# Later transposes, an earlier lambda and three later weight casts at the joint between the first feed-forward block and the token mixer

## The chip, the cores and the metric

The kernel runs on one core of one Trainium2 chip. The metric is device time in microseconds (us) of one execution. The kernel before took 925.24 us (median of three runs, from 924.72 to 927.66).

## The reference, cut to what matters

One layer in float32 on 512 tokens of width 1024: a feed-forward block (SwiGLU, 2816 hidden columns), a token mixer (attention), a second feed-forward block, and a last RMS norm. In four of the mixer's heads two softmaxes are combined with a scalar, `lam`. The mixer's input is the first block's output, normed over the 1024 columns; its first step is the projection to queries, keys and values.

```
def swiglu(x, w_gate, w_up, w_down):
    return (jax.nn.silu(x @ w_gate) * (x @ w_up)) @ w_down
...
    proj = h @ w_in
...
    lam = (jnp.exp(jnp.sum(lq1.astype(f32) * lk1.astype(f32)))
           - jnp.exp(jnp.sum(lq2.astype(f32) * lk2.astype(f32))) + lam0)
...
        a = p[:, :, 0] - lam * p[:, :, 1]
...
        x = x + 0.5 * swiglu(rmsnorm(x, ffn1_norm[layer]),
                             ffn1_w_gate[layer], ffn1_w_up[layer], ffn1_w_down[layer])
        x = x + token_mixer(rmsnorm(x, mix_norm[layer]), w_in[layer], w_out[layer],
...
    return rmsnorm(x, final_norm)
```

## The kernel before, in words

**Precision.** Every large product is made of three matmuls of fp32r parts (`mm3`, L160 to L162): high part by high part, the activation's low part by the weight's high part, and high by the weight's low part. So each weight and each activation is split on the way: ScalarE (ACT in the profile) casts a high part `h`, and VectorE (DVE) subtracts it from the original for a low part `l`. TensorE (PE) needs both before it can use the operand.

**The first block's down projection** turns tokens to the outside (the result has 128 tokens on the partitions). Of the 22 blocks of 128 hidden rows the last sixteen are taken as eight pairs, in two groups of four pairs, each multiplied Strassen-like in seven products instead of eight. The second group (unit `("t", 1)`, four row pairs p = 0 to 3) runs the products `a11, a22, s2, a12, s1, s3, s4` in this order, each with four weight tiles. For each weight tile a small planner (`block_events`) pushes timed events on a heap: the load (L478, L484, L481), a sum if the product needs one (`total`, L406), the cast (`high`, L443) four steps ahead of the product and the low part (`low`, L447) three steps ahead; a step is the time of one tile's matmuls, 1.41 us in the plan. The heap's order is the order of the instructions on the engines; nothing is moved by a scheduler, so each engine executes its list in order and stands when an entry has to wait. In the same stretch the last hidden rows' own parts are still made (names `g0a`, `g1a`, and `h0a` to `h6a`, where `h5a` and `h6a` are the high and low part that product `a22` needs of the last row pair).

**The joint** is written by hand in `seam`. Its four token tiles tt = 0 to 3 each go through: two times nine matmuls of the first six row blocks, for the right half of the columns (`plain_mm`, out `pc`), an add to the stream (`add`, L1321, DVE), a sum of squares (`squared`, L1324, ACT), the norm's factor (`mean` and `root_part`, L1287 to L1295), a scaling (`scaled`, out `y`: one half on ACT L1332, one on DVE L1334), and eight 128x128 transposes on PE (`turn`, L1342, out `xt`). Tiles 0 and 1 fill four PSUM banks (side 0, 256 tokens), tiles 2 and 3 four banks (side 1). After the second turn of a side, `split` reads each bank twice per row block k = 0 to 7: ACT makes `xh` (L1281), DVE `xl` (L1283). The pool `mm` has four banks in all, so the first turn of side 1 writes the banks that side 0's `split` reads: bank k // 2 is free once both readers of its two row blocks are done.

Among the turns stand sixteen **chunks**: chunks 0 to 7 multiply side 0 by the first two units of query and key weights (`pq`, `pk`; chunk c reads row blocks 2(c mod 4) and the next, with unit c // 4), chunks 8 to 15 the same for side 1. A chunk is twelve matmuls. Each runs `step(c)`, which also issues what a table holds for that step (`put(step, rank, function)`): loads and splits of later weights (`raw_vw`, L1449 and L1453), the evacuation of finished units (`evac_now` for unit 0 at step 11: L1553, L1217, L1556, L1220, L1610; `casts_k`, `evac_k` and so on for unit 1 from step 16), the scores of the attention from step 16 on (`sc`, L1659 and L1660, in two PSUM banks in turn, each read by DVE at L1662), and the scalar **lambda**: `lam_load` (a GpSimd DMA of `lt` into a buffer that `y` of tile 2 held, L1395) and `lam` (two DVE operations on `lt`, an Exp on ACT with its table load at L1404, five small DVE operations).

Before the change the turn of tile 2 stands ahead of chunk 1, that of tile 3 ahead of chunk 4 with side 1's `split` behind it; lambda's load stands in step 6 and its arithmetic in step 14. Because chunk bodies come after their step's events of rank under 10, "in step 14" puts lambda's DVE and ACT work behind the evacuation of unit 0.

Of the kernel before, what the change touches and what calls it, by code (L numbers as in the profile page):

```python
# [57 lines left out]
          "seven": (("a11", "w", "b11"), ("a22", "z", "t4"), ("s2", "w", "t2"), ("a12", "v", "b21"),  # L58
                    ("s1", "z", "t1"), ("s3", "v", "t3"), ("s4", "z", "b22")),
          "fresh": ("a11", "a22", "s3"),  # L60
          "s1": ((8, 9, 10, 11),) * 2, "s3": (tuple(t[0] for t in PAIR_SLOTS),) * 2,
          "a22": (("bc", "ob", "ob", "sq"),) * 2, "a12": (("bc", "ob", "ob", "sq"),) * 2,
          "ahead": {"s1": ((26, 23, 20, 17),) * 2, "s3": ((-1.7, -2.7, -3.7, -4.7),) * 2,
                    "a11": ((11, 10, 9, 8), (11, 10, 5.9, 5.8)), "a22": ((8, 7.5, 7, 6.5), (6.5, 6.3, 3.8, 0.5)),
                    "a12": ((-1.6, -2.6, -3.6, -4.6),) * 2}},
    "b": {"plain": 4, "pairs": ((4, 6, 8, 10), (12, 14, 16, 18, 20)),
          "sets": {4: (28, 29, 30, 31, 32, 33, 34), 6: (35, 36, 37, 38, 39, 40, 41),
# [19 lines left out]
STEP, TILES_STEP = 1410, 5440  # L87
# [12 lines left out]
def tile_macaron(ctx: ExitStack, tc, xs, xT, wf, wgu1, wst1, wdg1, wqk, wvw, wv, wo, wgu2, wst2,  # L100
# [17 lines left out]
    def mm_bank(nm):  # L118
        return pp.tile([P, S], F32, tag="mm", name=nm, bufs=4)
# [39 lines left out]
    def mm3(po, wh, wl, mh, ml, first, last, on=False):  # L159
        T.matmul(po, wh, mh, start=first, stop=False, skip_group_check=on)  # L160
        T.matmul(po, wh, ml, start=False, stop=False, skip_group_check=on)  # L161
        T.matmul(po, wl, mh, start=False, stop=last, skip_group_check=on)  # L162
# [78 lines left out]
    def ffn(wgu, wst, wdg, n0, n1, norm, early, res, nm, hooks, first=None,  # L241
# [99 lines left out]
        shape = TURNED[nm]  # L341
# [171 lines left out]
        def at(time, rank, f, *a):  # L513
            count[0] += 1
            heapq.heappush(events, (time, rank, count[0], f, a))
# [335 lines left out]
        def block_events(t):  # L851
            u, o, p = ops[t]
            now = starts[t]
            if o[0] in shape["ahead"]:
                at(starts[begin[u]] - shape["ahead"][o[0]][u[1]][p] * STEP, 2.2, block_load, u, o[0], p)
            elif o[0] in ("a12", "a22"):
                at(now - 8 * STEP, 1.5, block_load, u, o[0], p)
            if final is not None and (u[1], o[0]) == (1, "s4"):
                now = starts[begin[u]] + (TURNED_KEPT[p] + 5) * STEP
            if o[0] in ("s2", "s4"):  # L860
                at(now - 5 * STEP, 2, total, t)
            at(now - 4 * STEP, 3, high, t)
            at(now - 3 * STEP, 2.5, low, t)
            if t == begin[u] and u[1] == 1 and final is not None:
                at(now + 2 * STEP, 1, final, "begin", now + 2 * STEP, put, None)
# [200 lines left out]
        for j in range(j0, n1):  # L1066
# [9 lines left out]
            for hf in range(2):  # L1076
                wh, wl = get_w(wgu[j, hf], f"gu{nm}{j}_{hf}")
                for kk in range(4):
                    k = hf * 4 + kk
                    for c, pt in ((0, pg), (1, pu)):  # L1080
                        o = kk * 256 + c * P
# [39 lines left out]
    with tc.manual_schedule(engines={mybir.EngineType.DVE, mybir.EngineType.Activation}):  # L1121
        for t in range(4):
            raw = wp.tile([P, 1024], F32, tag="raw", name=f"raw_f{t}")
            h, l = w_place()
            for kk in range(2):
                k = 2 * t + kk
                c = slice(kk * 512, kk * 512 + 512)
# [82 lines left out]
    def number(n, tt):  # L1210
        return fin[:, n * NQ + tt:n * NQ + tt + 1]

    def first_sum(tt):
        V.tensor_scalar(number(2, tt), number(0, tt), 1.0 / D, EPS, op0=ALU.mult, op1=ALU.add)
# [82 lines left out]
    def seam(step):  # L1297

        todo, now, ys, ts, cb = [], [0.0], {}, {}, {}

        def ev(t, f, *a):
            todo.append((t, len(todo), f, a))

        def pe(cost, f, *a):
            ev(now[0], f, *a)
            now[0] += cost

        def plain_mm(tt, hf):
            ah, al = closing["tiles"]
            if hf == 0:  # L1310
                tag = ("s", "s", "t", "t")[tt]
                cb[tt] = pp.tile([P, S], F32, tag=tag, name=f"pc{tt}", bufs=2)[:]
            c = slice(tt * P, (tt + 1) * P)
            for j in range(3 * hf, 3 * hf + 3):
                h, l = closing[j // 2]
                w = slice(j % 2 * 512, (j % 2 + 1) * 512)
                mm3(cb[tt], ah[j][:, c], al[j][:, c], h[:, w], l[:, w], j == 0, j == PLAIN - 1)

        def add(tt):
            y = x[4 + tt]  # L1320
            V.scalar_tensor_tensor(y, cb[tt], 0.5, y, op0=ALU.mult, op1=ALU.add)  # L1321

        def squared(dh, tt):
            A.activation(sq[:], x[4 * dh + tt], AF.Square, accum_out=number(dh, tt))  # L1324
            if dh == 0:
                first_sum(tt)

        def scaled(dh, tt):
            y = tp.tile([P, S], F32, tag=("ob", "ptb")[tt % 2], name=f"y{dh}{tt}")
            ys[dh, tt] = y  # L1330
            if dh == 0:
                A.activation(y[:], x[tt], AF.Copy, scale=number(6, tt))  # L1332
            else:
                V.tensor_scalar_mul(y[:], x[4 + tt], number(6, tt))  # L1334

        def turn(tt):
            side = tt // 2
            if tt % 2 == 0:
                ts[side] = [mm_bank(f"xt{side}{i}") for i in range(4)]
            for k in range(KD):  # L1340
                o = k % 2 * HS + tt % 2 * P
                T.transpose(ts[side][k // 2][:, o:o + P], ys[k // 4, tt][:, k % 4 * P:(k % 4 + 1) * P], ident[:])  # L1342

        def chain(tt):
            t = now[0]
            ev(t + 0.1, add, tt)
            ev(t + 0.8, squared, 1, tt)
            ev(t + 1.6, mean, tt)
            ev(t + 2.0, root_part, tt)
            for dh in range(2):  # L1350
                ev(t + 2.7, scaled, dh, tt)

        def split(side, t):
            for k in range(KD):
                ev(t + 0.1 + 0.42 * k, gathered, "h", 1, side, k, ts)
                ev(t + 0.55 + 0.42 * k, gathered, "l", 1, side, k, ts)

        ev(-1, V.tensor_scalar_mul, sm[:, KD:2 * KD], sm[:, KD:2 * KD], 2.0)
        for t, tt in ((0.2, 0), (0.9, 1), (2.9, 2), (3.6, 3)):
            ev(t, squared, 0, tt)  # L1360
        for t, low, u, hf, c, n in ((1.6, 2.7, 0, 0, 0, 1024), (8.1, 11.4, 0, 1, 0, 1024), (11.8, 12.5, 1, 0, 0, 512),
                                    (12.4, 13.1, 1, 0, 512, 512), (21.5, 22.1, 1, 1, 0, 512),
                                    (22.1, 22.7, 1, 1, 512, 512)):
            ev(t, early_high, u, hf, c, n)
            ev(low, early_low, u, hf, c, n)
        ev(0.3, early_load, 1, 0)
        ev(3.5, early_load, 1, 1)
        for tt in range(NQ):
            pe(2.05, plain_mm, tt, 0)
            if tt > 1:  # L1370
                pe(0.8, turn, tt - 2)
            if tt == 3:
                split(0, now[0])
            pe(2.05, plain_mm, tt, 1)
            chain(tt)
        for c in range(16):
            if c in (1, 4):
                pe(0.8, turn, 2 + c // 4)
            if c == 4:
                split(1, now[0])  # L1380
            pe(1.36, step, c)
        for _, _, f, a in sorted(todo, key=lambda e: (e[0], e[1])):
            f(*a)
# [46 lines left out]
    def put(t, rank, f, *a):  # L1430
        at.setdefault(t, []).append((rank, f, a))
# [8 lines left out]
    loaded, ready, later = {}, {}, []  # L1440
# [447 lines left out]
    for i, f in enumerate(bounds):  # L1888
        put(22 + i, 9, f)

    put(6, 4, lam_load)
    put(14, 4, lam)
    for n, c in enumerate((0, 0, 2)):
        put(c, 0, load, n)
    for n, c in enumerate((3, 5)):
# [3 lines left out]
    def step(t):  # L1899
# [12 lines left out]
        if later:  # L1912
            hi_, lo_ = later.pop(0)
            hi_()
            lows.append(lo_)

    seam(step)
    for t in range(16, max(len(chunks), max(at) + 1)):
        step(t)
# [252 lines left out]
```

## Time and profile before

| | |
|---|---|
| timed runs | 924.72, 925.24, 927.66 us |
| the profiled execution | 923.94 us |
| its span, first to last instruction | 922.2 us |
| mean granted TensorE clock | 0.999 |
| TensorE busy | 911.1 us (99%), 5796 matmuls |
| VectorE busy | 716.1 us (78%) |
| ScalarE busy | 551.2 us (60%) |
| GpSimd busy | 93.3 us (10%) |
| the joint (chunks 0 to 15 and the turns among them) | from 344.1 to 371.1 us |
| the second down group begins | 287.6 us |

The profile's rows of a timeline read: start in us, duration in us, engine, line of the kernel, operation, out<-in, shape, count, and in brackets the idle time of the engine just before it with what ended it. PEld is TensorE's loading of the stationary operand, which runs beside the matmuls. SPq is the queue of the engine that issues most loads. Matmuls are pipelined, so what a matmul costs is the time from its start to the next one's start (0.23 us at 512 columns, 0.12 us at 256), and not the duration in its row.

### The profile page before, as it was taken

The page shows a single profiled execution, that of the slowest core. Times are in us where ns is not written, and L with a number is a line of the kernel's source. Part 1 is how long each engine was busy: PE and PEld are TensorE (multiplying, and loading weights), DVE is VectorE, ACT ScalarE, POOL GpSimd, SP SyncE. Part 2 cuts the span into 40 slices and gives each one's busy share as a digit, 9 for nine tenths or more (in the row PEclk, how much of TensorE's full clock was granted, in tenths as well). Part 3 has the DMA queues.
Part 4 walks back from the last instruction along what each step waited for, and adds up shares of the span by engine and source line. Part 5 has one row for each costly group of instructions (what it writes and reads, how often), then busy time and mean ns, then how long its engine had stood idle before and what let it go on. Part 6 is the DMA issues. An engine that isn't in the chain of part 4 may idle for free.

```text
span 922.2 us, 15983 instructions
## 1 busy us (share of the span) xinstructions
PE 911.1 (99%) x5796; PEld 820.7 (89%) x5796; DVE 716.1 (78%) x1486; ACT 551.2 (60%) x1160; POOL 93.3 (10%) x117
## 2 busy tenths in 40 slices
PE   9999999999999999999999999999999999999997
PEld 7888999889998889888989878989999889999885
DVE  7797887687888964857866546797887877988786
ACT  7454665445657564655776675656666446666563
POOL 0001111112120000000000000011221012211100
PEclk9999999999999999999999999999999999999999
DMA  7456679567895642324444204365798269787722
GB/s 256 125 140 158 181 181 261 137 153 199 188 229 156 168 137 76 92 92 116 137 111 118 69 23 138 93 149 161 186 240 214 81 182 236 206 187 208 194 69 91
DMA packets 65807, 141.52 MB, mean 153 GB/s; under 512 B 7552, under 2 KB 8064, under 8 KB 65728
## 3 DMA queue, kind: packets, MB, share of 16 engines
q1 hardware_dynamic: 50736, 113.02, 38.0%
q0 software_dynamic: 14992, 27.48, 18.4%
q8 instruction: 45, 0.74, 0.3%
q14 instruction: 34, 0.28, 0.1%
HBM read 135.20 MB, written 2.14 MB: 149 GB/s over the span
## 4 chain that ended last, share of the span: by engine, by line
PE 92%; DVE 4%; ACT 2%; issue 1%; DMA 0%; DVEq 0%; SPq 0%; ACTq 0%
PE pt L162 5%; PE pt L160 5%; PE pt L161 5%; PE pwo L160 2%; PE pwo L161 2%; PE pwo L162 2%; PE pq L160 2%; PE pua L160 2%; PE pua L162 2%; PE pua L161 2%; PE pq L161 1%; PE pq L162 1%; PE pk L160 1%; PE pk L162 1%; PE pk L161 1%; PE pp L160 1%
## 5 line engine op out<-in xcount | busy, mean ns | idle before, releaser
L1665 ACT ACTIVATE pr<-pr,mx 128x128 f32<-128x128 f32 (+3 forms) x64 | 36.0, 563 | 36.4 <-DVE mx L1662 36.1
L1662 DVE CUSTOM_DVE_ANT_0 pr<-sc,strip 128x128 f32<-128x128 f32 (+3 forms) x64 | 30.5, 489 | 21.8 <-PE sc L1660 21.3
L379 POOL DMA_DIRECT2D s1bg<-wst_dram x10 | 8.7, 865 | 352.8 <-DVE fin L1294 239.1
L535 DVE SCALAR_TENSOR_TENSOR x<-pt,x 128x512 f32<-128x512 f32 x50 | 32.8, 687 | 14.1 <-PE pt L162 11.7
L447 DVE TENSOR_TENSOR w<-s2b,w 128x512 fp32r<-128x512 f32 x38 | 26.1, 687 | 6.0 <-ACT w L443 6.0
L443 ACT CAST w<-s2b 128x512 fp32r<-128x512 f32 x38 | 23.6, 620 | 6.4 <-DVE s2b L411 6.1
L160 PE MATMUL pwo<-w,mh 128*128 128x512 f32 x64 | 25.9, 405 | 0.0
L447 DVE TENSOR_TENSOR w<-s2a,w 128x512 fp32r<-128x512 f32 x30 | 20.6, 687 | 6.5 <-ACT w L443 6.5
L161 PE MATMUL pwo<-w,mh 128*128 128x512 f32 x64 | 25.0, 391 | 0.0
L162 PE MATMUL pwo<-w,ml 128*128 128x512 f32 x64 | 25.0, 391 | 0.0
L443 ACT CAST w<-s2a 128x512 fp32r<-128x512 f32 x30 | 18.6, 620 | 8.0 <-DVE s2a L411 8.0
L443 ACT CAST w<-raa 128x512 fp32r<-128x512 f32 x24 | 14.5, 621 | 13.8 <-PE pt L162 5.6
L162 PE MATMUL pwgb<-xh,w 128*128 128x256 f32 x80 | 22.7, 284 | 0.0
L1453 DVE TENSOR_TENSOR w<-raw_qk,w 128x512 fp32r<-128x512 f32 x24 | 16.4, 687 | 8.1 <-ACT w L1449 8.0
L160 PE MATMUL pwgb<-xh,w 128*128 128x256 f32 x80 | 22.5, 281 | 0.0
L161 PE MATMUL pxgb<-ttb,w 128*128 128x256 f32 x80 | 22.5, 281 | 0.0
L161 PE MATMUL pwgb<-xl,w 128*128 128x256 f32 x80 | 22.5, 281 | 0.0
L1659 PE MATMUL sc<-k,q 128*128 128x128 f32 (+3 forms) x64 | 20.7, 325 | 0.8 <-DVE mx L1662 0.8
L1660 PE MATMUL sc<-l,q 128*128 128x128 f32 (+3 forms) x64 | 20.4, 322 | 0.0
L162 PE MATMUL pwub<-xh,w 128*128 128x256 f32 x72 | 20.3, 281 | 0.0
L161 PE MATMUL pwub<-xl,w 128*128 128x256 f32 x72 | 20.3, 281 | 0.0
L160 PE MATMUL pwub<-xh,w 128*128 128x256 f32 x72 | 20.3, 281 | 0.0
(728 smaller groups left out, 3868.3 us busy)
## 6 DMA issues: line engine op xcount, KB each, us to landing
raw_qk<-wqk_dram SPq DMA_DIRECT2D x12, 512.0 KB, 3.5
raw0bg<-wst_dram SPq DMA_DIRECT2D x10, 512.0 KB, 5.5
raw0bu<-wst_dram SPq DMA_DIRECT2D x9, 512.0 KB, 5.9
raw_gua<-wgu_dram SPq DMA_DIRECT2D x8, 512.0 KB, 3.7
raw0ag<-wst_dram SPq DMA_DIRECT2D x8, 512.0 KB, 5.1
strip<-bias_rows SPq DMA_DIRECT2D x16, 256.0 KB, 3.6
raw_wo<-wo_dram SPq DMA_DIRECT2D x8, 512.0 KB, 3.5
raw0au<-wst_dram SPq DMA_DIRECT2D x7, 512.0 KB, 6.7
```

The source lines that it names most:

```text
L160: T.matmul(po, wh, mh, start=first, stop=False, skip_group_check=on)
L161: T.matmul(po, wh, ml, start=False, stop=False, skip_group_check=on)
L162: T.matmul(po, wl, mh, start=False, stop=last, skip_group_check=on)
L379: nc.gpsimd.dma_start(t[:], b, accum_op=ALU.add)
L443: A.copy(made[t][0], source(t))
L447: V.tensor_tensor(l, source(t), h.bitcast(F32), op=ALU.subtract)
L535: V.scalar_tensor_tensor(o, a, f, b, op0=ALU.mult, op1=op1)
L1453: V.tensor_tensor(l[:, c:c + 512], raw[:, c:c + 512], h[:, c:c + 512].bitcast(F32), op=ALU.subtract)
L1659: T.matmul(ps[:, :w], qs[:, qi], ks[:, :w], start=True, stop=False)
L1660: T.matmul(ps[:, :w], qs[:, qi], ls[:, :w], start=False, stop=True)
L1662: V.tensor_tensor_reduce(out=pi, in0=ps[:, :w], in1=st["b"][m][:, w - 1::-1], op0=ALU.add, op1=ALU.min, scale=1.0, scalar=3.0e38, accum_ou ...
L1665: A.activation(pi, pi, AF.Exp, scale=-1.0, bias=st["mx"][:, m, i:i + 1], accum_out=st["ls"][:, m, i:i + 1])
```

## The change

Four things move; nothing is added and nothing taken away.

```
+          "later": ((("t", 1), "a11", 2), (("t", 1), "a11", 3), (("t", 1), "a22", 3)),
...
-                    "a12": ((-1.6, -2.6, -3.6, -4.6),) * 2}},
+                    "a12": ((-1.6, -2.6, -3.6, -4.6), (-1.6, -2.6, -3.6, -5.2))}},
...
+            if (u, o[0], p) in shape.get("later", ()):
+                now += STEP
             at(now - 4 * STEP, 3, high, t)
             at(now - 3 * STEP, 2.5, low, t)
...
         for c in range(16):
-            if c in (1, 4):
-                pe(0.8, turn, 2 + c // 4)
-            if c == 4:
+            if c in (3, 5):
+                pe(0.8, turn, 2 + c // 5)
+            if c == 5:
                 split(1, now[0])
             pe(1.36, step, c)
...
-    put(6, 4, lam_load)
-    put(14, 4, lam)
+    put(4, 4, lam_load)
+    put(9, 4, lam)
```

The turn of tile 2 goes from ahead of chunk 1 to ahead of chunk 3, that of tile 3 from ahead of chunk 4 to ahead of chunk 5, and `split(1)` with it. Lambda's load goes from step 6 to step 4, its arithmetic from step 14 to step 9. In the second down group the casts and low parts of `a11` p = 2 and 3 and of `a22` p = 3 go one step later, and the load of `a12` p = 3, which uses the buffer (`sq`) of `a22` p = 3, 0.6 steps later. Line numbers of the changed kernel are 1 higher from the table on and 3 higher behind `block_events`.

On PE, in the joint: the last matmul of chunk 0, the turn of tile 2 (`y_3695` and `y_3697` are its two halves, `xt_3743` to `xt_3746` the four banks), and the first of chunk 1, before.

```order
L162 MATMUL pk_3722<-xh_79,wql_3569 128x256
L1342 MATMUL xt_3743<-ident,y_3695 128x128 x2
L1342 MATMUL xt_3744<-ident,y_3695 128x128 x2
L1342 MATMUL xt_3745<-ident,y_3697 128x128 x2
L1342 MATMUL xt_3746<-ident,y_3697 128x128 x2
L160 MATMUL pq_3721<-xh_80,wqh_3568 128x256
```

The same turn on PE in the changed kernel stands between the last matmul of chunk 2 (row block 5 is `xh_83`) and the first of chunk 3 (row block 6 is `xh_84`).

```order
L163 MATMUL pk_3722<-xh_83,wx 128x256
L1345 MATMUL xt_3782<-ident,y_3695 128x128 x2
L1345 MATMUL xt_3783<-ident,y_3695 128x128 x2
L1345 MATMUL xt_3784<-ident,y_3697 128x128 x2
L1345 MATMUL xt_3785<-ident,y_3697 128x128 x2
L161 MATMUL pq_3721<-xh_84,wqh_3617 128x256
```

So the 24 matmuls of chunks 1 and 2 went ahead of it.

On ACT, from side 1's last `xh` on: the evacuation of unit 0 (`q_3943` to `l_3948`), lambda's table load and Exp, and the first casts of unit 1's keys (`k_4034`, `k_4035`) and the first softmax exponential, before.

```order
L1281 ACTIVATE xh_85<-xt_3746,x_104 128x256
L1553 ACTIVATE q_3943<-pq_3721 64x512
L1217 CAST k_3945<-pk_3722 64x512 x2
L1610 CAST l_3947<-l_3947 64x512
L1553 ACTIVATE q_3944<-pq_3721 64x512
L1217 CAST k_3946<-pk_3722 64x512 x2
L1610 CAST l_3948<-l_3948 64x512
L1404 ACT_TABLE_LOAD
L1404 ACTIVATE ls<-ls 128x2
L1217 CAST k_4034<-pk_3821 64x512
L1217 CAST k_4035<-pk_3821 64x512
L1665 ACTIVATE pr_3977,ls_3980<-pr_3977,mx_3979 128x128
```

The same stretch on ACT in the changed kernel.

```order
L1284 ACTIVATE xh_85<-xt_3785,x_104 128x256
L1407 ACT_TABLE_LOAD
L1407 ACTIVATE ls<-ls 128x2
L1556 ACTIVATE q_3954<-pq_3721 64x512
L1220 CAST k_3956<-pk_3722 64x512 x2
L1613 CAST l_3958<-l_3958 64x512
L1556 ACTIVATE q_3955<-pq_3721 64x512
L1220 CAST k_3957<-pk_3722 64x512 x2
L1613 CAST l_3959<-l_3959 64x512
L1220 CAST k_4034<-pk_3815 64x512
L1220 CAST k_4035<-pk_3815 64x512
L1668 ACTIVATE pr_3988,ls_3991<-pr_3988,mx_3990 128x128
```

The table load and the Exp went from between the two units' evacuations to ahead of both; on DVE lambda's seven operations went the same way, from ahead of the first L1662 to right behind side 1's last `xl`.

On DVE, in the second down group: a sum for `s2` (`raa`), the low part of `a22` p = 3 (`w<-sq`), and the parts `h4a` and `h6a` of the last row pair, before.

```order
L406 TENSOR_TENSOR raa_3025<-sCa_2792,raa_3025 128x512
L447 TENSOR_TENSOR w<-sq,w 128x512
L715 TENSOR_TENSOR h4a_3319<-g0a_3063,h3a_3258 128x512
L406 TENSOR_TENSOR raa_3136<-sCa_2859,raa_3136 128x512
L447 TENSOR_TENSOR w<-raa_3025,w 128x512
L1191 TENSOR_TENSOR ac<-ac,rb 16x16
L715 TENSOR_TENSOR h6a_3335<-g1a_3096,h5a_3294 128x512
```

The same rows on DVE in the changed kernel.

```order
L407 TENSOR_TENSOR raa_3025<-sCa_2792,raa_3025 128x512
L716 TENSOR_TENSOR h4a_3317<-g0a_3063,h3a_3258 128x512
L407 TENSOR_TENSOR raa_3136<-sCa_2859,raa_3136 128x512
L448 TENSOR_TENSOR w<-sq,w 128x512
L448 TENSOR_TENSOR w<-raa_3025,w 128x512
L1194 TENSOR_TENSOR ac<-ac,rb 16x16
L716 TENSOR_TENSOR h6a_3335<-g1a_3096,h5a_3293 128x512
```

The low part from `sq` went two places back, and `h6a` kept its place. The two `a11` low parts likewise went three and two places back further up. On ACT the cast of `sq` went behind three bias operations (L1187), the cast of `h5a` and two copies of the finished product `a11` (L523), the cast of `a11` p = 3 behind two casts of the last rows' parts; on SP the load of `a12` p = 3 changed places with the load that followed it.

## The prediction

> **What bounds the kernel now.** First the page's busy line, then all waits of TensorE (PE).
>
> ```profile
> PE 911.1 (99%) x5796; PEld 820.7 (89%) x5796; DVE 716.1 (78%) x1486; ACT 551.2 (60%) x1160; POOL 93.3 (10%) x117
> ```
>
> ```profile
> PE warm L1112 <- POOL ones_d L1106: 1.0, 1, 1.0
> PE xt L1342 <- DVE fin L1287: 0.9, 1, 0.9
> PE pga L1157 <- ACT w L1137: 0.9, 1, 0.9
> PE sc L1659 <- DVE mx L1662: 0.8, 1, 0.8
> PE xt L1342 <- DVE xl L1283: 0.6, 1, 0.6
> ```
>
> PE is the bound nearly everywhere. Five waits make all of its idle time, 4.2 us; two lie at the program's start, out of the change's reach. The other three lie in the joint and at the first scores, 2.3 us by this list. Work on other engines counts only where PE ends up waiting. A "busy" PE also includes stalls that the pipelined ends cover, so I read the price from the starts of PE's rows: the turn of tile 2, which begins where chunk 0 ends, the next chunk's first matmul, and for comparison the turn of tile 3, three chunks on.
>
> ```profile
> 345.81 0.60 PE L1342 MATMUL xt<-ident,y 128*128 128x128 f32 x4
> 347.06 0.41 PE L1342 MATMUL xt<-ident,y 128*128 128x128 f32 x2 [0.65 <-DVE xl L1283]
> 348.36 0.41 PE L1342 MATMUL xt<-ident,y 128*128 128x128 f32 x2 [0.89 <-DVE fin L1287]
> 348.52 0.36 PE L160 MATMUL pq<-xh,wqh 128*128 128x256 f32 x1
> ...
> 352.93 1.03 PE L1342 MATMUL xt<-ident,y 128*128 128x128 f32 x8
> 353.72 0.36 PE L160 MATMUL pq<-xh,wqh 128*128 128x256 f32 x1
> ```
>
> The turn of tile 3 costs 353.72 - 352.93 = 0.79 us, that of tile 2 348.52 - 345.81 = 2.71: **1.92 us too many**. What does it wait for? The third bank, then the fourth. DVE's side of it (`xl` of side 0, with tile 3's `add` between) and ACT's last `xh`:
>
> ```profile
> 343.87 1.66 DVE L1283 SCALAR_TENSOR_TENSOR xl<-xt,x,xh 128x256 fp32r<-128x256 f32 x4 [1.06 <-ACT xh L1281]
> 345.44 0.68 DVE L1321 SCALAR_TENSOR_TENSOR x<-pc,x 128x512 f32<-128x512 f32 x1
> 346.04 0.87 DVE L1283 SCALAR_TENSOR_TENSOR xl<-xt,x,xh 128x256 fp32r<-128x256 f32 x2
> 347.33 0.88 DVE L1283 SCALAR_TENSOR_TENSOR xl<-xt,x,xh 128x256 fp32r<-128x256 f32 x2 [0.43 <-ACT xh L1281]
> ```
>
> ```profile
> 346.22 0.63 ACT L1324 ACTIVATE sq<-x 128x512 f32<-128x512 f32 x1 [0.56 <-DVE x L1321]
> ...
> 346.85 0.46 ACT L1281 ACTIVATE xh<-xt,x 128x256 fp32r<-128x256 f32 x1
> ```
>
> The first six `xl` end at 346.91 and the third pair of transposes starts at 347.06; the last two end at 348.21 and the fourth pair starts at 348.36. The reader that frees a bank lets PE in 0.15 us later (the name `fin` in the list is the operation after it).
>
> **The turn, 1.92 us.** The end at 348.21 hangs on ACT's square at 346.22 and that on `add` at 345.44, whose matmuls ended before chunk 0. None of it depends on where the turn stands, so in the new place the same bank is free at 348.36. A chunk costs (352.93 - 348.52) / 3 = 1.47 us. Chunks 1 and 2, now first, start at 345.81 and end at 348.75. Chunk 1 reads `xl` 2 and 3, ready at 345.53; chunk 2 reads 4 and 5 from 347.28, ready at 346.91; chunk 3 reads 6 and 7 after the turn, ready at 348.21. So the turn starts at 348.75 with every bank free, its first by 4 us, its last (used about 0.4 into the turn) by 0.8, and ends at 349.54. Chunks 3 and 4 follow, and the turn of tile 3 stands at 352.48. Its `y` comes from here:
>
> ```profile
> 349.19 0.72 ACT L1332 ACTIVATE y<-x,fin 128x512 f32<-128x512 f32 x1 [0.68 <-DVE fin L1295]
> ...
> 353.34 1.20 ACT L1281 ACTIVATE xh<-xt,x 128x256 fp32r<-128x256 f32 x3 [1.35 <-PE xt L1342]
> ```
>
> It is there at 349.91. I count the whole 1.92 as gained. What is late next? Side 1's split has one chunk less of cover. ACT starts it 0.41 after the turn (353.34 against 352.93), so at 352.89; eight `xh` at 0.40 and the one weight cast now between them (0.5) end at 356.6, and DVE, 0.9 behind at first, needs eight at 0.40 and two low parts at 0.6: about 358. Chunk 8 starts at 353.27 + 3 x 1.47 = 357.68 and needs only the first two pairs, chunk 11 at 362.1 the last. About 3 us of cover stay: 0.
>
> **Lambda, 1.04 us.** The first scores (`sc`), with PE's rows around the wait:
>
> ```profile
> 377.30 0.40 PE L1518 MATMUL pvw<-w,xh 128*128 128x512 f32 x1
> 378.46 0.44 PE L1659 MATMUL sc<-k,q 128*128 128x384 f32 x1 [0.76 <-DVE mx L1662]
> 378.74 0.34 PE L1660 MATMUL sc<-l,q 128*128 128x384 f32 x1
> 378.91 0.40 PE L1516 MATMUL pvw<-w,xh 128*128 128x512 f32 x1
> ```
>
> From 377.30 to 378.46 are 1.16 instead of the 0.23 of such a matmul, then 0.28 for the first `sc` where the second, of the same shape, takes 0.17: 0.93 + 0.11 = 1.04 lost. PE wants the bank that DVE reads in L1662, in this string:
>
> ```profile
> 370.61 0.29 DVE L1401 TENSOR_TENSOR lp<-lt 128x128 f32<-128x128 f32 x1
> ...
> 373.74 0.29 DVE L1662 CUSTOM_DVE_ANT_0 pr<-sc,strip 128x128 f32<-128x128 f32 x1
> ...
> 378.32 0.08 DVE L1662 DVE_READ_ACCUMULATOR2_ANT mx<- 128x1 f32 x1
> ```
>
> ```profile
> 371.25 1.28 ACT L1404 ACT_TABLE_LOAD   x1
> ...
> 372.78 1.19 ACT L1217 CAST k<-pk 64x512 fp32r<-64x512 f32 x2
> ```
>
> Lambda holds DVE from 370.61 to 373.7 and ACT from 371.25 to 372.78. Without it the casts of `k`, whose bank PE fills four chunks after chunk 11 (below: 365.15 + 4 x 1.47 = 371.0), start at about 371.3, 1.5 earlier. DVE's first L1662 moves by more, since its score follows chunk 15 at once, and what stands between it and 378.32 are ACT's casts and DVE's answers to them, all 1.5 earlier. A string moved by 1.5 clears a wait of 0.93. Relative to PE I count 1.04 gained. In its new place lambda falls into this hole:
>
> ```profile
> 365.15 0.59 ACT L1553 ACTIVATE q<-pq 64x512 fp32r<-64x512 f32 x1 [7.75 <-PE pq L162]
> 365.78 0.68 DVE L1556 SCALAR_TENSOR_TENSOR q<-pq,q 64x512 fp32r<-64x512 f32 x1 [6.54 <-ACT q L1553]
> ```
>
> ACT starts unit 0's evacuation there when PE is through chunk 11, in the new kernel at 365.15 - 1.92 = 363.2. Lambda needs 3.1 from about 358, so it ends near 361.1, with 2 us to spare.
>
> ```profile
> 346.98 0.58 POOL L1395 DMA_DIRECT2D lt<-lams_dram  x1 [40.62 <-PE xt L1342]
> ...
> DMA to landing us min/median/max: 3.5/3.5/3.5
> ```
>
> Its input waits for `y` of tile 2 to be read by PE, then near 349.2, and lands 3.5 later, at 352.7; nothing else is queued on GpSimd there.
>
> **The three casts, 0.** In the second down group PE's weight load stands 0.39 us once, for a residual that DVE makes late (the group's first row, then PEld's, DVE's and ACT's):
>
> ```profile
> 287.60 0.40 PE L160 MATMUL pt<-w,h0a 128*128 128x512 f32 x1
> ```
>
> ```profile
> 297.74 0.19 PEld L162 LDWEIGHTS pt<-w,h6a 128*128 128x128 f32 x1 [0.39 <-DVE h6a L715]
> ```
>
> ```profile
> 294.52 0.69 DVE L447 TENSOR_TENSOR w<-sq,w 128x512 fp32r<-128x512 f32 x1
> ```
>
> ```profile
> 294.47 1.04 ACT L523 COPY pt<-pt 128x512 f32<-128x512 f32 x2
> ```
>
> All that stood ahead of `h6a` on DVE still does, and DVE works there without a gap, so it ends when it did. The new risk is that `w<-sq`, on DVE now two places of 0.6 later, at 295.7, waits for ACT's cast behind the copies. With that cast gone from ahead of them the copies can start when PE is through `a11`, near 287.6 + 4 x 1.4 = 293.2, and the cast is done at 295.0. Were the copies to keep their time and end at 295.5, the cast would end at 296.1, and `h6a` and PE come 0.4 later. Bounds: -0.39 (the wait goes) to +0.4; I take 0, since the rows ahead of `h6a` are the same. The load that shares `sq` leaves 0.8 later on SP, behind one load more:
>
> ```profile
> 295.62 0.38 SPq L481 DMA_DIRECT2D sq<-wdg_dram  x1
> ...
> 302.79 0.62 ACT L443 CAST w<-sq 128x512 fp32r<-128x512 f32 x1 [1.28 <-DMA sq<-wdg_dram]
> ```
>
> Its product starts near 287.6 + 15 x 1.4 = 308.6, 4 us after the cast would now end: 0.
>
> **The sum.** 1.92 + 1.04 = 2.96. The profiled execution took 923.94 (span 922.2 and 1.74 around it), so 920.98; the median of the timed runs lies 1.30 higher, 925.24, and gives **922.3**. Behind that I see nothing that takes it back or adds to it, for DVE has caught up with PE soon after in the kernel before, too:
>
> ```profile
> 388.62 0.56 DVE L1662 CUSTOM_DVE_ANT_0 pr<-sc,strip 128x384 f32<-128x384 f32 x1 [0.92 <-PE sc L1660]
> ```
>
> **The rivals.** (a) *The scores still wait.* If the string at 371 to 378 hangs on PE's own rhythm (DVE's `q` and weight parts) rather than on lambda, only the turn is gained: 923.3. For it: DVE has work in every slice there. Against it: 1.5 of shift for a wait of 0.93. 0.12. (b) *The wait moves along with the turn*, the change not doing what it says, if the banks' readers slipped behind the two chunks: only lambda's 1.04, 924.2. Against it the chain of rows above, which ends at 348.21 without a link to chunks 1 or 2. 0.05. (c) *Slower: lambda's input comes late.* ACT is in order, so an Exp without its input holds unit 0's evacuation. With lambda's last 2.5 us behind the landing, it harms nothing up to a landing at about 360.7; scores need that evacuation 1.5 later, and from there PE stands one to one. To eat 2.96 the load would have to land after 365, 16 us after its issue against 3.5; at 20 us PE would stand 7.0, 929.3. 0.03. The Trainium skill (DMA: Bandwidth & Descriptors, "SWDGE vs HWDGE vs iDMA") speaks for this rival: GpSimd writes the descriptors of its DMAs into a part of SBUF from which VectorE locks it out in a two-port mode, and the load now issues beside VectorE's scaling of tile 3 and seven splits. The trace of before shows no such hold: VectorE was busy from 347.33 beside the load's issue, and it landed after 3.5; what VectorE ran there, though, read PSUM. Held until VectorE rests at 358, it would land at 361.5, and PE would still lose nothing or little.
>
> **How the numbers follow.** Forecast 0.80, (a) 0.12, (b) 0.05, (c) 0.03. About 0.3% of the time, 2.78 us, is what a measurement can tell from no change. My 2.96 stands hardly beyond it; the casts' bounds (2.56 to 3.35) and the scatter of medians, about 0.5 by the two close runs 924.72 and 925.24, leave two thirds of the forecast's 0.80 beyond: faster 0.53, with little from (a). Slower by as much: (c) and a little for a larger stall at the casts, 0.04. Within: 0.43. The range: 925.24 - 3.35 - two such scatters gives 920.9, and (b)'s 924.2 with half a scatter 924.5.
>
> **What would show it.** Right: the turn of tile 2 at about 0.8 us without a wait behind chunk 2; the table load inside ACT's idle stretch near 357 to 361; no PE wait on L1662; the wait on `h6a` unchanged. Wrong: a wait on `xl` in chunks 1 or 2 or at chunk 8, a PE wait at L1659, a longer one on `h6a`, or 2.96 gained in the joint and lost behind it.

## The result, and the profile after

The changed kernel takes 921.20 us (median of nine runs, 920.30 to 922.71), the kernel before beside it 924.54 (nine runs, 923.29 to 927.66): ratio 0.9964, 95% interval 0.9953 to 0.9975, so 2.3 to 4.3 us of 924.54 are gained, 3.34 by the medians. The profiled execution took 921.00 with a span of 919.2, against 923.94 and 922.2: 2.94 less. Forecast were 922.3 and a gain of 2.96.

First the page's busy line, then all waits of TensorE (PE) after the change.

```profile
PE 911.2 (99%) x5796; PEld 821.5 (89%) x5796; DVE 716.4 (78%) x1486; ACT 551.5 (60%) x1160; POOL 93.3 (10%) x117
```

```profile
PE warm L1115 <- POOL ones_d L1109: 1.0, 1, 1.0
PE pt L1753 <- ACT ptx L1755: 0.2, 1, 0.2
```

PE has the same 911 us of work; what went is idle time. Both waits on `xt` and the one on `sc` are gone. The 0.9 on `pga` at the program's start is missing too, but that is scatter and no part of the gain: it is back with 0.2 to 0.6 in most of the other runs below, with and without the change, and chunk 0 begins no earlier than before. The wait on `pt` (0.2) is none of the change's: in the trace of before, PE has a gap of 0.32 at 398.87 that the list of waits does not name. PE's rows, at the turn of tile 2 with the first matmul of chunk 3, and at the scores that used to stand:

```profile
348.90 1.04 PE L1345 MATMUL xt<-ident,y 128*128 128x128 f32 x8
349.69 0.36 PE L161 MATMUL pq<-xh,wqh 128*128 128x256 f32 x1
...
375.56 0.39 PE L1521 MATMUL pvw<-w,xh 128*128 128x512 f32 x1
375.79 0.33 PE L1662 MATMUL sc<-k,q 128*128 128x384 f32 x1
375.96 0.34 PE L1663 MATMUL sc<-l,q 128*128 128x384 f32 x1
```

The turn of tile 2 costs 349.69 - 348.90 = 0.79, as that of tile 3 always did; before it cost 2.71, so 1.92 are gone. From the `pvw` to the second `sc` are 375.96 - 375.56 = 0.40, before 378.74 - 377.30 = 1.44, so 1.04 are gone. Both are the terms of the sum to the hundredth. Where else did time go? The second `sc` stands at 375.96 instead of 378.74, 2.78 earlier, although chunk 0 began 0.19 later than before (344.32 against the 344.13 at the joint's start): 2.97 gained between the two, and the span ends 3.0 earlier. Nothing behind the joint gave it back. (That the profiled executions differ by just the forecast's amount is partly luck: their joints happen to begin only 0.19 apart, see the last section.)

Now the engines that PE waited for. DVE, at the last low parts of side 0 and of side 1, and at lambda's first and last operation:

```profile
347.54 0.88 DVE L1286 SCALAR_TENSOR_TENSOR xl<-xt,x,xh 128x256 fp32r<-128x256 f32 x2 [0.43 <-ACT xh L1284]
...
357.49 0.87 DVE L1286 SCALAR_TENSOR_TENSOR xl<-xt,x,xh 128x256 fp32r<-128x256 f32 x2
358.28 0.28 DVE L1404 TENSOR_TENSOR lp<-lt 128x128 f32<-128x128 f32 x1
...
359.92 0.16 DVE L1413 TENSOR_TENSOR nlam<-nlam,keep 128x1 f32<-128x1 f32 x1
```

The last `xl` of side 0 still end where they did relative to the program (348.42, before 348.21, with the joint 0.19 later): nothing in the split became faster. The turn now comes 0.5 after that end instead of 2.4 before it. ACT, at the same places and at the first casts of unit 1's keys:

```profile
354.65 1.96 ACT L1284 ACTIVATE xh<-xt,x 128x256 fp32r<-128x256 f32 x5
356.63 1.28 ACT L1407 ACT_TABLE_LOAD   x1
358.92 0.20 ACT L1407 ACTIVATE ls<-ls 128x2 f32<-128x2 f32 x1 [1.00 <-DVE ls L1406]
363.42 0.59 ACT L1556 ACTIVATE q<-pq 64x512 fp32r<-64x512 f32 x1 [4.30 <-PE pq L163]
...
369.54 1.19 ACT L1220 CAST k<-pk 64x512 fp32r<-64x512 f32 x2
```

The table load stands at the start of an idle stretch, and 4.3 us of it are left behind the Exp. The casts of `k` start at 369.54 instead of 372.78, that is 3.24 earlier: 1.7 with PE (the 1.92 less the joint's 0.19), and 1.5 of its own, which is the shift that the forecast gave this string.

### The profile page after: what moved, and what is told of

It reads as the page before. It is cut to its first block, busy times and chain, and to the rows that moved or that the text cites. A ratio compares the mean times of both kernels' runs of the same rounds, so it can differ in the third digit from the quotient of the medians.

```text
span 919.2 us, 15980 instructions
## 1 busy us (share of the span) xinstructions
PE 911.2 (99%) x5796; PEld 821.5 (89%) x5796; DVE 716.4 (78%) x1486; ACT 551.5 (60%) x1160; POOL 93.3 (10%) x117
## 4 chain that ended last, share of the span: by engine, by line
PE 96%; DVE 2%; ACT 1%; issue 1%; DVEq 0%; POOL 0%; ACTq 0%; POOLq 0%
PE pt L163 5%; PE pt L161 5%; PE pt L162 5%; PE pq L161 2%; PE pwo L161 2%; PE pq L162 2%; PE pq L163 2%; PE pk L161 2%; PE pk L163 2%; PE pk L162 2%; PE pwo L162 2%; PE pwo L163 2%; PE pua L163 2%; PE pua L161 2%; PE pua L162 2%; PE pp L161 1%
## 5 line engine op out<-in xcount | busy, mean ns | idle before, releaser
L1662 PE MATMUL sc<-k,q 128*128 128x128 f32 (+3 forms) x64 | 20.5, 322 | 0.0
L162 PE MATMUL pxub<-ttb,w 128*128 128x256 f32 x72 | 20.2, 281 | 0.0
```

The source lines that it names most:

```text
L1662: T.matmul(ps[:, :w], qs[:, qi], ks[:, :w], start=True, stop=False)
```

## The experiments

Each was timed in five rounds beside the kernel before; kernels with the same time of before in the table shared a chip and those runs of before. Theory: the turn's bank wait (1.92) and the scores' wait behind lambda (1.04) are two separate stalls, worth their length each, and the casts are worth nothing.

| kernel | what differs | us | before, same chip | ratio, 95% interval |
|---|---|---|---|---|
| e1_turns | only the turns moved | 922.24 | 923.86 | 0.9982 (0.9974 to 0.9991) |
| e2_lambda | only lambda moved | 923.33 | 923.86 | 0.9992 (0.9984 to 1.0001) |
| e3_casts | only the casts moved | 924.03 | 923.86 | 1.0000 (0.9991 to 1.0008) |
| e4_no_casts | turns and lambda | 921.24 | 923.86 | 0.9968 (0.9956 to 0.9979) |
| e5_turn_at_2 | turn of tile 2 ahead of chunk 2 | 921.54 | 923.97 | 0.9973 (0.9962 to 0.9985) |
| e6_table_only | turns, and the table load alone early | 921.15 | 923.97 | 0.9971 (0.9961 to 0.9982) |
| e7_h6a_first | the change, `h6a` earlier on DVE | 921.11 | 923.97 | 0.9968 (0.9955 to 0.9980) |
| e8_lambda_12 | turns, lambda in step 12 | 921.79 | 923.97 | 0.9979 (0.9970 to 0.9987) |
| e9_scale_late | the change, tile 2 scaled later | 920.74 | 924.54 | 0.9964 (0.9950 to 0.9978) |
| e10_all_three | the change, three more stalls removed | 920.19 | 924.54 | 0.9954 (0.9940 to 0.9967) |
| e11_change_again | the change itself once more | 921.88 | 924.54 | 0.9970 (0.9956 to 0.9983) |

### The parts alone

**e1_turns.** The kernel before with only this:

```
-            if c in (1, 4):
-                pe(0.8, turn, 2 + c // 4)
-            if c == 4:
+            if c in (3, 5):
+                pe(0.8, turn, 2 + c // 5)
+            if c == 5:
                 split(1, now[0])
```

> Only the two turns and side 1's split are moved; lambda and the casts stay as before. Theory (two separate stalls): the turn of tile 2 falls from 2.71 us to about 0.8, the wait of the scores on DVE stays at about 1.04, and the kernel is 1.9 us faster than before (ratio near 0.998). Rival (one stall makes the other, through DVE and ACT falling behind in the joint): the scores' wait goes as well, and the kernel is 3.0 us faster (0.9968).

0.9982, 1.66 us of 923.86. PE's rows of this kernel: the turn in its new place, and the scores.

```profile
348.06 1.03 PE L1342 MATMUL xt<-ident,y 128*128 128x128 f32 x8
...
374.74 0.39 PE L1518 MATMUL pvw<-w,xh 128*128 128x512 f32 x1
375.88 0.44 PE L1659 MATMUL sc<-k,q 128*128 128x384 f32 x1 [0.75 <-DVE mx L1662]
376.16 0.34 PE L1660 MATMUL sc<-l,q 128*128 128x384 f32 x1
```

The turn waits for nothing, and the scores' stall is whole: 376.16 - 374.74 = 1.42, against 0.40 without it. The two stalls do not depend on each other.

**e2_lambda.** The kernel before with `put(4, 4, lam_load)` and `put(9, 4, lam)`.

> Only lambda's load and arithmetic are moved; turns and casts stay as before. Theory: the turn of tile 2 keeps its 2.71 us, no wait of PE at L1659, 1.0 us faster than before (ratio near 0.9989). Rival (the scores hang on PE's own rhythm, lambda does not matter, and in the changed kernel it was the turns that cleared them): the wait at L1659 stays near 1 us and the time stays within 0.3 us of before.

0.9992, 0.7 us; the interval, from 1.5 gained to 0.1 lost, holds both 1.04 and 0. The rows decide: the turn as before, the scores free.

```profile
346.59 0.41 PE L1342 MATMUL xt<-ident,y 128*128 128x128 f32 x2 [0.64 <-DVE xl L1283]
347.89 0.41 PE L1342 MATMUL xt<-ident,y 128*128 128x128 f32 x2 [0.90 <-DVE fin L1287]
...
376.83 0.39 PE L1518 MATMUL pvw<-w,xh 128*128 128x512 f32 x1
377.05 0.33 PE L1659 MATMUL sc<-k,q 128*128 128x384 f32 x1
```

**e3_casts.** The kernel before with only the casts' part of the table:

```
+          "later": ((("t", 1), "a11", 2), (("t", 1), "a11", 3), (("t", 1), "a22", 3)),
...
+                    "a12": ((-1.6, -2.6, -3.6, -4.6), (-1.6, -2.6, -3.6, -5.2))}},
...
+            if (u, o[0], p) in shape.get("later", ()):
+                now += STEP
```

> Only the three casts, their low parts and the one load are moved. Theory: 0; PE's weight load for h6a still stands about 0.4 us, the turn and the scores wait as before. Rival (the casts give what the measured gain has over the 2.96 worked out, 0.4): that stand goes and the kernel is 0.4 us faster; the other way, the later load of the fourth a12 tile costs up to 0.4.

1.0000, at most 0.9 either way, and PE's weight load is stalled as it was (0.39 before):

```profile
297.98 0.19 PEld L163 LDWEIGHTS pt<-w,h6a 128*128 128x128 f32 x1 [0.41 <-DVE h6a L716]
```

**e4_no_casts.** The changed kernel without these lines.

> Turns and lambda are moved as in the change, the casts stay as before. Theory: all of the change's gain, 3.0 to 3.3 us faster than before (ratio 0.9964 to 0.9968), and the same PE rows in the joint as the whole change. Rival (the casts matter): 2.6 us faster or less.

0.9968, 3.0 us: the whole gain without the casts. The parts alone give 1.66 + 0.7 + 0 = 2.4, together 3.0, the same within their intervals. The traces tell it more sharply. From the first matmul of chunk 0 to the second score of 384 columns (`sc<-l,q`) are 34.61 us before, 32.66 in e1_turns, 33.55 in e2_lambda, 34.60 in e3_casts, 31.62 in e4_no_casts, and 31.64 and 31.63 in the two profiles of the change (the second is e11_change_again): 1.95 and 1.06 for the parts, 0.01 for the casts, 2.97 together.

### Why the turn waits: bank by bank

**e5_turn_at_2.** The changed kernel with the turn of tile 2 one chunk earlier:

```
-            if c in (3, 5):
+            if c in (2, 5):
                 pe(0.8, turn, 2 + c // 5)
```

> The changed kernel with the turn of tile 2 ahead of chunk 2 instead of chunk 3. Theory (each bank is freed by its own last reader): the turn begins when chunk 1 ends, three pairs of transposes run at once and only the fourth waits, about 0.5 us, so 2.5 us faster than before (0.9973). Rival (the turn as a whole waits for the last reader of side 0): no transpose before the last xl has ended, 1.1 us lost, 1.9 us faster than before (0.9980).

```profile
346.56 0.82 PE L1345 MATMUL xt<-ident,y 128*128 128x128 f32 x6
347.65 0.41 PE L1345 MATMUL xt<-ident,y 128*128 128x128 f32 x2 [0.28 <-DVE fin L1290]
347.82 0.36 PE L161 MATMUL pq<-xh,wqh 128*128 128x256 f32 x1
```

Six transposes pass, only the last pair stands: 347.82 - 346.56 = 1.26 instead of 0.79, 0.47 lost. DVE's first six `xl` ended at 346.20, before the turn, and the last two at 347.51, 0.14 before the last pair. So a bank is given back as soon as its own two readers are done, and one chunk of shift buys about three quarters of the stall, two buy all. The time, 921.54, cannot tell this from the change; the rows can.

### Why the scores wait: where the table load stands

**e6_table_only.** Casts as before, turns moved, lambda's arithmetic left in step 14; new is an Exp of a constant column in step 9, into a scratch column, which only draws ACT's table load ahead.

```
-    put(4, 4, lam_load)
-    put(9, 4, lam)
+    put(6, 4, lam_load)
+    put(9, 4, A.activation, root[:], eps[:], AF.Exp)
+    put(14, 4, lam)
```

> The turns moved as in the change, the casts as before, and of lambda only the table load: one Exp of a one-column constant is put into step 9 so that the table is there, and lambda's arithmetic stays in step 14. Theory (the 1.28 us of the table load on ACT, which hold the casts of k, are enough to make the wait): no wait or under 0.1 us at L1659, 3.0 us faster than before (0.9968). Rival (DVE's seven operations, about 1.9 us in front of the first L1662, hold the string as well): a wait of 0.5 us or more stays, 2.5 us faster or less (0.9973).

ACT's rows, then PE's at the scores:

```profile
357.88 1.28 ACT L1904 ACT_TABLE_LOAD   x1
...
370.78 0.20 ACT L1404 ACTIVATE ls<-ls 128x2 f32<-128x2 f32 x1
371.01 1.19 ACT L1217 CAST k<-pk 64x512 fp32r<-64x512 f32 x2
```

```profile
376.81 0.39 PE L1518 MATMUL pvw<-w,xh 128*128 128x512 f32 x1
377.04 0.33 PE L1659 MATMUL sc<-k,q 128*128 128x384 f32 x1
```

No stall, although lambda's arithmetic, DVE's seven small operations among it, stands where it stood. The change moves all of lambda; to remove the stall it is enough to move the 1.28 us of the table load. (This profile runs some 1.3 us late all along, 377.04 where the changed kernel has 375.79, which is no part of the edit; see the last section.)

**e8_lambda_12.** Turns moved, casts as before, lambda earlier than before but behind ACT's idle stretch: `put(12, 4, lam)`.

> Turns moved as in the change, casts as before, lambda's arithmetic in step 12, between the two halves of unit 0's evacuation: earlier than before, but not in the stretch where ACT and DVE stand idle. Theory (it is the idle stretch that counts, not the earlier place): ACT's second half of the evacuation and the casts of k behind it come 1.5 us later, the wait at L1659 is back at about 1 us, and 1.9 us faster than before (0.9980). Rival (any place ahead of the casts of k will do): no wait, 3.0 us faster (0.9968).

ACT, DVE at unit 0's second `q`, then PE at the first scores and at those of 384 columns:

```profile
365.95 1.28 ACT L1404 ACT_TABLE_LOAD   x1
367.25 0.20 ACT L1404 ACTIVATE ls<-ls 128x2 f32<-128x2 f32 x1
...
368.44 0.69 DVE L1556 SCALAR_TENSOR_TENSOR q<-pq,q 64x512 fp32r<-64x512 f32 x1
```

```profile
368.72 0.28 PE L162 MATMUL pk<-xh,wql 128*128 128x256 f32 x1
369.28 0.30 PE L1659 MATMUL sc<-k,q 128*128 128x128 f32 x1 [0.28 <-DVE q L1556]
...
375.56 0.39 PE L1518 MATMUL pvw<-w,xh 128*128 128x512 f32 x1
376.16 0.44 PE L1659 MATMUL sc<-k,q 128*128 128x384 f32 x1 [0.21 <-DVE mx L1662]
376.44 0.34 PE L1660 MATMUL sc<-l,q 128*128 128x384 f32 x1
```

The stall is back in two pieces: 369.28 - 368.72 = 0.56 where 0.12 is regular, and 376.44 - 375.56 = 0.88 where 0.40 is, in sum 0.92. Only the second is the wait of before. The first is a wait for unit 0's second `q`: ACT's part of it was done at 368.07, but DVE was held until 368.41 by lambda's small operations, which themselves had waited for the Exp behind the load. So "earlier" alone buys only about 0.1 of the 1.04; where the stall is gone whole, in the change and in e6_table_only, the load falls where ACT has nothing to do.

### Three stalls more

**e7_h6a_first.** The changed kernel with the low part of the second group's `h6a` three places earlier on DVE:

```
-            at(n + 4 * STEP + late, 1, t1_rest)
+            at(n + (4 if j < JF - 2 or final is not None else 3) * STEP + late, 2.1, t1_rest)
```

> The changed kernel with the low part h6a of the last row pair three places earlier on DVE, ahead of the low part from sq. Theory (h6a stands late only because of its place in DVE's list): the stand of PE's weight load for h6a goes, PE gains 0.25 us in that place, 3.2 to 3.5 us faster than before (0.9962 to 0.9965), hardly to be told from the change by time alone. Rival: PE waits for the low part from sq instead and nothing is gained.

The stall of the weight load is gone; PE's rows step by 0.22 to 0.23 from 296.00 to 299.17. For the time, 921.11, the quarter of a microsecond is too small to be seen.

**e9_scale_late.** The changed kernel with `scaled` of tile 2 behind the first of side 0's splits:

```
-                ev(t + 2.7, scaled, dh, tt)
+                ev(t + (3.9 if tt == 2 else 2.7), scaled, dh, tt)
```

> The change, with one step more: the scaling of the residual of token tile 2 (DVE's 0.68 us ahead of side 0's splits) is put 1.2 steps later, behind the first three high parts and two low parts of side 0. Theory (a later turn needs tile 2's scaled tokens only at about 348.9, so the splits may go ahead of it): the first xh starts about 1.3 us earlier, the low parts about 0.6 us, TensorE's remaining 0.17 us in chunk 0 goes, and the time is about 3.1 us below before, 0.2 us below the change, which is within the scatter. Rival (the scaling is wanted earlier than that): the turn of tile 2 gets a wait on y, and the time is 0.3 to 1 us above the change.

The rows are the theory's: chunk 0 starts 343.47, 343.58, 343.70, without the extra step, and PE has no wait on `xt`. The distance from chunk 0 to the second score is 31.37 instead of 31.64, so 0.27 are gained there.

**e10_all_three.** Both of these, and the transposes of unit 0's last tile behind their chunk:

```
-            put(tv - 2, 2, turn, ((3,),))
+            put(tv - 2, 2 if u else 10, turn, ((3,),))
```

> The change with three small waits more taken away: the scaling later, as in the run beside it; the low part of the second group's h6a three places earlier on DVE; and the transposes of unit 0's last tile behind their chunk, where they now wait for ACT's copy (0.33 us at 395). Theory (each stall that TensorE shows is worth its length, and they add up): 0.2 + 0.25 + 0.33 us on top of the change's 2.9, about 3.7 us below before, a ratio near 0.996, and none of the three left in the profile. Rival (such small stalls are made good by later slack): the time of the change, 2.9 us below before.

**e11_change_again.** The changed kernel unchanged.

> The change itself, timed again beside the other two on the same chip: 2.9 us below before, the ratio between 0.9955 and 0.9975 by both theories. It tells how far two measurements of one kernel lie apart, against which the 0.2 and 0.8 us of the others are read.

PE's rows in e10_all_three, at chunk 0 and at unit 0's transposes, and then the same places of the changed kernel:

```profile
343.09 0.28 PE L161 MATMUL pq<-xh,wqh 128*128 128x256 f32 x1
343.20 0.28 PE L162 MATMUL pq<-xl,wqh 128*128 128x256 f32 x1
...
395.34 0.39 PE L1521 MATMUL pvw<-w,xh 128*128 128x512 f32 x1
395.58 0.60 PE L1753 MATMUL pt<-ident,pr 128*128 128x128 f32 x4
```

```profile
344.32 0.28 PE L161 MATMUL pq<-xh,wqh 128*128 128x256 f32 x1
344.61 0.39 PE L162 MATMUL pq<-xl,wqh 128*128 128x256 f32 x1
...
395.47 0.40 PE L1521 MATMUL pvw<-w,xh 128*128 128x512 f32 x1
396.03 0.66 PE L1753 MATMUL pt<-ident,pr 128*128 128x128 f32 x4 [0.17 <-ACT ptx L1755]
```

0.29 became 0.11 (with the step behind it 0.27 are gained in chunk 0), and 0.56 became 0.24. All three stalls are gone, and e10_all_three, at 920.19, is the fastest kernel of the study: 0.9954, 3.1 to 5.5 us below before. Against the change timed beside it (921.88) it is 1.7 faster by the medians, of which the three stalls explain 0.8, but the two intervals overlap: that it beats the change is likely by its rows, and not shown by the time. Two measurements of the change, 0.9964 and 0.9970, lie 0.6 us apart, nearly as much as the three stalls are worth. e9_scale_late's 920.74 says no more.

## Why the prediction was right

**The turn, 1.92.** Right in size and in reason. The step "none of it depends on where the turn stands, so in the new place the same bank is free" is what the rows show: last `xl` done at 348.42, turn started at 348.90 without a wait (forecast 348.75; 348.94 with the joint's 0.19). e1_turns shows it without the other parts, and e5_turn_at_2 confirms the freeing bank by bank. Rival (b), the wait that moves along, is refuted by the same rows.

**The cover of side 1's split, 0.** Right: ACT's last `xh` ended at 356.61 (forecast 356.6), DVE's last `xl` at 358.36 (about 358), and PE stood nowhere in chunks 8 to 15.

**Lambda, 1.04.** Right in size. That a string moved by 1.5 clears a wait of 0.93 held, and rival (a) is refuted. But the prediction priced lambda as one block on DVE and ACT; e6_table_only shows that moving the table load alone removes the stall, and e8_lambda_12 that a smaller move would have left a stall of 0.92. Lambda itself ended at 360.08, not near 361.1: the table load ran beside DVE's last splits (from 356.63, before the Exp had its input), so that only 1.8 of the 3.1 us stood behind them.

Here a rule bears on the size. The Trainium skill (ScalarE: Activation LUTs, "What ACT_TABLE_LOAD costs") gives 1283 ns for the load and some 1380 ns more for a drain, 2.66 us per change of table. The load's row agrees (1.28). The drain shows on neither side of it in e8_lambda_12: the cast ahead ended at 365.94 and the Exp stands at 367.25, behind 365.95 + 1.28. On 1.28 + 0.2, and not on 2.66, the forecast's 1.5 of shift rested.

**The casts, 0.** Right: e3_casts measures nothing, and the wait on `h6a` is as long as before. ACT went as worked out; its rows of the changed kernel:

```profile
293.53 1.04 ACT L524 COPY pt<-pt 128x512 f32<-128x512 f32 x2
294.52 0.62 ACT L444 CAST w<-sq 128x512 fp32r<-128x512 f32 x1
...
304.27 0.62 ACT L444 CAST w<-sq 128x512 fp32r<-128x512 f32 x1 [2.57 <-DMA sq<-wdg_dram]
```

The copies start at 293.53 (forecast near 293.2) and the cast is done at 295.14 (295.0). One thing the forecast had too small: the cast of `sq` that waits for the moved load starts at 304.27, 1.5 later than before where 0.8 was counted. The load left 1.0 later (296.62 instead of 295.62), which is the 0.8 and the 0.19 by which this program runs later; the rest is that it took 7.5 to land instead of 7.1. Two copies queue behind the cast. DVE waits for them:

```profile
305.41 1.29 DVE L536 SCALAR_TENSOR_TENSOR x<-pt,x 128x512 f32<-128x512 f32 x2 [0.98 <-ACT pt L524]
```

That wait is new, and PE does not see it: its matmuls start every 0.23 from 303.74 to 309.86.

**Lambda's input, rival (c).** Its row on GpSimd, and DVE's work beside it:

```profile
350.07 0.58 POOL L1398 DMA_DIRECT2D lt<-lams_dram  x1 [44.85 <-PE xt L1345]
```

```profile
349.40 0.49 DVE L1337 TENSOR_SCALAR y<-x,fin 128x512 f32<-128x512 f32 x1
350.67 1.29 DVE L1223 TENSOR_TENSOR wql<-raw_q,wqh 128x512 fp32r<-128x512 f32 x2 [0.78 <-ACT wqh L1220]
```

It was issued at 350.07, where 349.2 was forecast: 1.17 after the start of the turn, as before (346.98 - 345.81). It landed 3.5 after its issue, as before. By the rule that the prediction took from the Trainium skill (DMA: Bandwidth & Descriptors, "SWDGE vs HWDGE vs iDMA") VectorE would keep GpSimd from writing descriptors in a two-port mode. Here the scaling ended at 349.89, before the issue, and the next splits began at 350.67, when GpSimd was done with issuing it (350.65). (Weight splits beside side 1's `xl` were counted as seven; the rows show six.) A hold was not provoked, so the rule itself was not tried.

**The number.** The gain was right: 2.96, against 2.94 by the profile, 2.97 by the rows of the joint and 3.34 by the medians. The forecast lies 1.1 above the measured median: 0.7 of it because it was hung on the median of three runs, 925.24, where nine runs of the same kernel gave 924.54, and 0.4, the excess of 3.34 over 2.96, is within the scatter of the medians. So the reference, and not a term of the sum, made most of the error.

## What to carry to other kernels

Price a stall of the bounding engine by the start-to-start distance of its rows against the same operation without a wait, and look for a stretch of work that does not need the stalled result and can go in front: a stall so hidden is gained whole as long as the readers' chain does not hang on the moved work. A table load is such a piece of work on ScalarE: it did not wait for the input of its Exp (load at 356.63, input ready at 358.88), and an Exp of one column drew it into an idle stretch without moving the arithmetic that needs the table (e6_table_only). Stalls of 0.2 to 0.3 us add up in the rows (e10_all_three), but each alone lies within the scatter of the time, so they must be read from the trace.

## What the runs showed that was not expected

Much of the scatter of this kernel's time arises in its first 105 us. The last matmul of one product in the changed kernel, in e9_scale_late and in e6_table_only, which differ from each other only behind 280 us:

```profile
102.22 0.28 PE L163 MATMUL pxga<-tta,w 128*128 128x256 f32 x1
```

```profile
101.35 0.27 PE L163 MATMUL pxga<-tta,w 128*128 128x256 f32 x1
```

```profile
103.49 0.27 PE L162 MATMUL pxga<-tta,w 128*128 128x256 f32 x1
```

The same work stands up to 2.1 us apart, most of the 2.9 that the change is worth. e6_table_only's profiled execution took 923.47 where its median is 921.15, and it reaches this matmul 1.3 later than the changed kernel. In e10_all_three it stands at 101.29, 0.93 earlier than in the changed kernel: of the 1.9 by which its profile's span (917.3) is shorter than the changed kernel's (919.2), half comes from there and 0.8 from the three stalls. Two traces compared from a common matmul ahead of the edit are free of this; two spans are not. It needs a common matmul behind the edit, too: between 750 and 850 us PE has waits of 0.4 to 0.7 in e1_turns (1.1 in sum), e6_table_only and e8_lambda_12 that the kernel before and the change do not have there, far behind what was edited.
